# Opening a two-layer encoder by channel pairs, with the masks of its mLSTM on VectorE

## The chip, the cores and the metric

One core of one Trainium2 chip runs the kernel. The metric is the device time of one execution in microseconds (us). Five engines work side by side: TensorE (PE in the profile; PEld is its weight load), VectorE (DVE), ScalarE (ACT), GpSimd (POOL), and SyncE (SP), which here issues the DMAs.

## The reference, cut to what matters

Two independent sequences (a prompt of 256 tokens and a sample of 512, width 1024) go through two layers. Each layer's modulation (shift, scale and gate, for its mixer and its feed-forward part) comes from a condition vector. The first layer's mixer is a two-directional mLSTM with four heads of 256, the second's is a windowed attention; a convolutional feed-forward part follows each.

```python
def trunk(x, c, ...):
    for l in range(DEPTH):
        mod = jax.nn.silu(c) @ adaln_w[l] + adaln_b[l]
        sh1, sc1, g1, sh2, sc2, g2 = [t[:, None, :] for t in jnp.split(mod, 6, axis=-1)]
        h = rmsnorm(x, norm_g[l, 0]) * (1 + sc1) + sh1
        y = mlstm_mixer(h, ...)      # layer 0; swa_mixer in layer 1
        x = x + g1 * y
        h = rmsnorm(x, norm_g[l, 1]) * (1 + sc2) + sh2
        x = x + g2 * conv_ffn(h, ...)
    return rmsnorm(x, final_g)
```

In the mLSTM, `proj = h @ w_in` gives queries, keys, values, an output gate and, per head and direction, an input and a forget gate. With F the running sum of log forget gates, a = input gate - F and M the running maximum of a, the scores of a head are (k.q) * exp(a_s - M_t), for s up to t in one direction and from t on in the other. The kernel computes each direction as one masked matrix. Its outputs are divided by max(|sum of scores|, exp(-(F + M))), the two directions are added, and each head's row of 256 is normalised by its root mean square, scaled by `head_g` and multiplied by sigmoid(o).

## The kernel before, in words

The activations lie with channels on partitions: eight channel blocks `c` or `k` of 128, and 768 columns, prompt's 0 to 256 and the sample's 256 to 768. `SEQS` names the two sequences, q = 0 the sample and q = 1 the prompt; `RANGES` cuts the columns into three: r0 (256:512) and r1 (512:768) of the sample, r2 the prompt. Every matmul with a large weight is done on split operands: a high part in fp32r (`whi`, `hh`, a ScalarE cast) and a low part (`wlo`, `hl`, a VectorE subtraction), with three products hi x hi, hi x lo, lo x hi. `fp_copy_split` (L268) is the cast at L272 and the subtraction at L273. In the trace `hh` is `zh` and `hl` is `zl`. `split` (L287) makes a weight's parts of 128x1024 out of a `raw` tile, which `load` (L284) fetches with a DMA of 512 KB from SyncE's queue. The `raw` ring has 5 buffers, `whi` and `wlo` 3 each, the slabs (12 KB a partition) 6. TensorE's output goes to two sets of four PSUM banks, `ps` and `pa`.

`first` (L1561) opens the kernel. It loads the sample's x, streams the first third of the layer's modulation weights (`adaln`, L401: 16 chunks of 512 KB, each multiplied with the condition in `silc`), and meanwhile scales the two sample ranges by their RMS factors (`Norm`, L90, with `scaled`, L569). `adaln` ends with the copies of the result to `sb` (L431, L432; `sb` is a tile of the `raw` ring), four transposes (L435), shift and scale (`mod`, L442) and the gain (L445). Then `modulate` (L574) makes `hh` and `hl` of both ranges: eight modulations on VectorE (L578) and eight splits for each.

`mlstm` (L667) follows. It splits the first two query weights, loads prompt's x, squares prompt's channels on ScalarE (L111) and puts all eight sums of squares on TensorE (`Norm(..., KC)`, `pa<-inv,nt` in the trace). Prompt's RMS factor (its power is L160 on GpSimd) is spread over the partitions by TensorE (`pa<-kct,nr`) and applied in `modulated` (L561, L563, L564). `window` (L323) runs the gate weight and the two query weights over r0, r1 and r2: 3 x 3 x 8 x 3 matmuls of 256 columns. The decay follows (L699 to L716): log forget gates, running sums and maxima as scans on VectorE, and M written to DRAM.

For each head, M is broadcast from DRAM into a slab `mb` (L732). GpSimd adds the two masks for all blocks into its other half (L734). Queries and keys come from `gemmT`, values from `gemmN` (L344). For each of six score blocks ScalarE makes the exponentials (L793 to L797), and VectorE multiplies them with the scores (L798, L799). Then come the outputs: the products with the values, the denominator (L841 to L845), the two directions' sum `hs` (L846, L847), its square (L849). A half head (one sequence) closes with a power on GpSimd (L852), the scale (L855), transposes (L859) and the head's weight into `hsT` (L863).

Between these products two generators do other work step by step. `fillp` (`adaln_g`, L455) is the rest of the first layer's modulation, four groups of eight steps, on TensorE, with loads through the `raw` ring. `fill` (`adaln_v`, L497) is the second layer's, on VectorE (L516, L518). Head 0 takes four steps of `fillp` (two before the outputs of each half), heads 1 to 3 eleven each.

What sets the order: the code gives every instruction its priority, and a planner lets each engine take the first in this order that is ready in its own account of time and buffers. So the order on an engine can differ from the code's. A ring hands its buffers out in the code's order. Within an engine the order is then fixed: what waits holds up what stands behind it.

Of the kernel before, what the change touches and what calls it, by code (L numbers as in the profile page):

```python
# [16 lines left out]
P = 128  # L17
# [162 lines left out]
class Net:  # L180
# [116 lines left out]
    def ahead(self, u, h):  # L297

        self.early[u, h] = self.split(self.load(u, h))
# [44 lines left out]
    def gemmN(self, u, evac):  # L344

        ws = []
        for _, (hi, lo) in self.halves(u):
            ws.append((hi.rearrange("p (k m) -> p k m", k=4), lo.rearrange("p (k m) -> p k m", k=4)))
        for t in range(T // P):
# [50 lines left out]

    def adaln(self, l, th):  # L401
# [16 lines left out]
        ps = self.ps()  # L418
        for i in range(2 * KC):
            k, h = divmod(i, 2)  # L420
            cur = fetch(i)
            for g in range(2):
                r0 = 32 * (2 * h + g)
                self.mm(
                    ps[r0 : r0 + 32, :], self.silc[:, k, :], cur[:, g * 512 : (g + 1) * 512], k == 0, k == KC - 1
                )
# [4 lines left out]
        nc.vector.tensor_copy(sb[0], ps[:, :256])  # L431
        nc.scalar.copy(sb[1], ps[:, 256:])  # L432
        pt = self.ps()
        for b in range(4):
            nc.tensor.transpose(  # L435
                pt[:, b * P : (b + 1) * P], sb[b // 2][:, (b % 2) * P : (b % 2 + 1) * P], self.ident
            )
# [5 lines left out]
        if th == 0:  # L443
            for s in range(2):
# [52 lines left out]
    def adaln_v(self, l, pool):  # L497
# [9 lines left out]
        for grp, k in rows:  # L507
# [5 lines left out]
            for s in range(2):  # L513
                w = self.silc[:, k, s : s + 1]
                if k == 0:
                    nc.vector.tensor_scalar(acc[:, s], row, w, None, ALU.mult)  # L516
# [56 lines left out]

    def modulate(self, xt, rng, l, i):  # L574
        c0, c1, q = rng
        for c in range(KC):
            x = xt[c // 4][:, c % 4, c0:c1]
            self.nc.vector.tensor_scalar(  # L578
                x, x, self.gain[l][i][:, c, q : q + 1], self.mod[l][:, 24 * i + c, q : q + 1], ALU.mult, ALU.add
            )  # L580
            self.fp_copy_split(self.hh[:, c, c0:c1], self.hl[:, c, c0:c1], x)
# [85 lines left out]
    def mlstm(self, pool, gw, xt):  # L667
# [27 lines left out]
        for c in range(KC):  # L695
            norm.square(c)
        self.start(PROMPT, norm.stages())
        self.window(ws)
        nc.scalar.preload_act_table_set("natural_log_exp_and_others")  # L699
        nc.scalar.activation(ex, gf, AF.Abs)  # L700
        nc.scalar.activation(ex, ex, AF.Exp, scale=-1.0)
        nc.scalar.activation(ex, ex, AF.Ln, bias=self.ones[0:G, 0:1])
        nc.vector.tensor_scalar(lf, gf, 0.0, None, ALU.min)
        nc.vector.tensor_tensor(lf, lf, ex, ALU.subtract)
        scan = nc.vector.tensor_tensor_scan
        for s0, s1 in SEQS:
            scan(F[0:4, s0:s1], lf[0:4, s0:s1], z[0:4, s0:s1], 0.0, ALU.add, ALU.add)
            b = slice(s0, s1)
            scan(F[32:36, b][:, ::-1], lf[32:36, b][:, ::-1], z[32:36, b], 0.0, ALU.add, ALU.add)
        nc.vector.tensor_tensor(a, gi, F, ALU.subtract)  # L710
        for s0, s1 in SEQS:
            b = slice(s0, s1)
            scan(M[0:4, b], a[0:4, b], z[0:4, b], 0.0, ALU.max, ALU.add)
            scan(M[32:36, b][:, ::-1], a[32:36, b][:, ::-1], z[32:36, b], 0.0, ALU.max, ALU.add)
        md = self.dp.tile([G, T], F32, name="mrows")
        nc.sync.dma_start(md, M)  # L716
# [9 lines left out]
        hsT = [self.slab([P, 4, T]) for _ in range(2)]  # L726
        for h in range(4):

            mb = self.slab([P, 4, T])
            for d in range(2):  # L730
                r = d * 32 + h
                nc.sync.dma_start(mb[:, d], md[r : r + 1, :].to_broadcast([P, T]))  # L732
                mask = self.kct[:, (MF, MB)[d] : (MF, MB)[d] + P]
                nc.gpsimd.tensor_tensor(  # L734
                    mb[:, 2 + d].rearrange("p (t c) -> p t c", t=T6),
                    mb[:, d].rearrange("p (t c) -> p t c", t=T6),
                    mask.unsqueeze(1).to_broadcast([P, T6, P]),
                    ALU.add,
                )
            qk = []  # L740
            for i in range(2):
# [4 lines left out]
                for c, w in self.halves(U_MIN + 3 * h + i):  # L746
                    for q in range(2):
                        keep(t, i, c)(q, self.gemmT(w, q))
# [7 lines left out]
            def values():  # L756
# [4 lines left out]
                def evac(t, o):  # L761
                    self.fp_copy_split(v[:, 0, t, :256], v[:, 1, t, :256], o)
# [5 lines left out]
                self.gemmN(U_MIN + 3 * h + 2, evac)  # L768
# [7 lines left out]
            for q, (s0, s1) in enumerate(SEQS):  # L776
                n = (s1 - s0) // P
                for j in range(n):
# [12 lines left out]
                    act = nc.scalar.activation  # L791
                    if j:
# [19 lines left out]
            if h == 0:  # L812
                nc.vector.tensor_tensor(F, F, M, ALU.add)
# [899 lines left out]
```

## Time and profile before

| what | value |
|---|---|
| median of 3 runs | 1832.8 us (1829.74 to 1832.9) |
| the profiled execution | 1832.56 us |
| its span, first to last instruction | 1830.8 us |
| ScalarE's share of the span | 49% |
| GpSimd's share of the span | 26% |
| DMA moved | 184.47 MB, mean 101 GB/s |

The page gives an engine's busy time, its share of the span and its number of instructions. A matmul's end is modelled, and a busy TensorE may run at half clock. The row PEclk shows the granted clock in tenths for 40 slices of the span, where 9 stands for 90% and more. In groups of instructions, the numbers are the count, the busy time, the mean ns of one, and the engine's idle time before them with what ended it. In the timeline a row begins with its start and its time in us.

### The profile page before, as it was taken

What the parts mean: (1) busy time and instruction counts of PE and PEld (TensorE: products, weight loads), DVE (VectorE), ACT (ScalarE), POOL (GpSimd) and SP (SyncE); (2) the same over time, 40 slices, a digit from 0 to 9 for tenths busy, and PEclk for the clock granted to TensorE, in tenths of its full rate; (3) what the DMA queues carried; (4) which work ended last, traced back from release to release, by engine and by line L of the source; (5) the groups of instructions that cost most, each with busy time, mean ns of one, the idle gap of its engine ahead of it and who ended that gap; (6) DMA issues with size and microseconds to landing.
All of it is one profiled execution on the core that took longest, in us unless ns stands there. A gap on an engine that the chain in (4) does not pass through costs nothing.

```text
span 1830.8 us, 28867 instructions
## 1 busy us (share of the span) xinstructions
PE 1789.2 (98%) x11258; PEld 1653.6 (90%) x11258; DVE 1379.1 (75%) x2108; ACT 893.0 (49%) x1814; POOL 483.8 (26%) x385
## 2 busy tenths in 40 slices
PE   6999999999999999999999999999999999999998
PEld 3987887989998999999999999889989999999997
DVE  4755676886799877777777867767998777777876
ACT  4434434353556444444444566665564444444443
POOL 1001001022024333333331313430144333333321
PEclk7999999999999999999999999999999999999998
DMA  8344565546312222222222321124122222222212
GB/s 332 108 146 141 171 204 195 174 144 212 114 46 80 73 67 70 69 70 70 69 70 83 116 84 50 53 95 136 49 81 70 69 70 70 69 69 70 70 35 70
DMA packets 64244, 184.47 MB, mean 101 GB/s; under 512 B 6167, under 2 KB 23831, under 8 KB 64108
## 3 DMA queue, kind: packets, MB, share of 16 engines
q1 hardware_dynamic: 63532, 182.11, 30.3%
q8 instruction: 88, 1.44, 0.3%
q10 hardware_dynamic: 576, 0.52, 0.1%
q14 instruction: 48, 0.39, 0.1%
HBM read 176.17 MB, written 6.43 MB: 100 GB/s over the span
## 4 chain that ended last, share of the span: by engine, by line
PE 85%; DVE 5%; issue 4%; ACT 3%; DMA 1%; POOL 1%; SPq 0%; POOLq 0%; ACTq 0%; DVEq 0%
PE ps L266 27%; PE pa L266 24%; PE ps L1195 10%; PE ps L1196 10%; PE ps L1198 10%; PE pa L1034 1%; DVE wlo L273 1%; DMA slab<-in_adaln_w_dram 0%; DMA raw<-in_adaln_w_dram 0%; PE pa L1195 0%; PE pa L1196 0%; DVE ada L518 0%; ACT whi L272 0%; PE pa L1198 0%; ACT zh L1146 0%
## 5 line engine op out<-in xcount | busy, mean ns | idle before, releaser
L272 ACT CAST whi<-raw 128x1024 fp32r<-128x1024 f32 x233 | 243.8, 1049 | 332.5 <-PE pa L266 145.0
L273 DVE TENSOR_TENSOR wlo<-raw,whi 128x1024 fp32r<-128x1024 f32 x233 | 316.7, 1360 | 105.6 <-ACT whi L272 103.5
L266 PE MATMUL pa<-slab,whi 128*128 128x256 f32 (+1 forms) x1328 | 317.3, 334 | 0.0
L266 PEld LDWEIGHTS pa<-slab,whi 128*128 128x128 f32 x1328 | 230.1, 189 | 21.9 <-DVE slab L605 0.4
L605 DVE SCALAR_TENSOR_TENSOR slab<-pa,mod,slab 128x256 f32<-128x256 f32 (+1 forms) x332 | 192.7, 598 | 63.8 <-PE pa L266 63.6
L266 PE MATMUL pa<-slab,wlo 128*128 128x256 f32 (+1 forms) x664 | 212.8, 333 | 1.4 <-DVE wlo L273 1.4
L266 PE MATMUL ps<-zh,whi 128*128 128x256 f32 (+1 forms) x560 | 189.3, 339 | 2.6 <-ACT whi L272 1.9
L266 PE MATMUL ps<-zh,wlo 128*128 128x256 f32 (+1 forms) x560 | 184.1, 331 | 2.0 <-DVE wlo L273 2.0
L266 PE MATMUL ps<-zl,whi 128*128 128x256 f32 (+1 forms) x560 | 184.5, 332 | 0.5 <-DVE zl L564 0.5
L1195 PE MATMUL ps<-zh,whi 128*128 128x384 f32 x504 | 172.2, 342 | 3.8 <-ACT nt L1266 2.0
L1196 PE MATMUL ps<-zl,whi 128*128 128x384 f32 x504 | 169.9, 337 | 1.8 <-DVE zl L1152 1.8
L1198 PE MATMUL ps<-zh,wlo 128*128 128x384 f32 x504 | 169.0, 335 | 0.0
L266 PE MATMUL ps<-slab,whi 128*128 128x384 f32 (+2 forms) x656 | 163.5, 332 | 0.9 <-DVE slab L273 0.5
L266 PEld LDWEIGHTS pa<-slab,wlo 128*128 128x128 f32 x664 | 125.2, 189 | 14.3 <-DVE wlo L273 2.0
L1231 POOL TENSOR_TENSOR raw<-raw,raw 128x512 f32<-128x512 f32 x40 | 53.7, 1343 | 318.5 <-DVE wlo L273 245.8
L1447 POOL TENSOR_TENSOR slab<-slab 128x772 f32<-128x772 f32 x44 | 87.0, 1978 | 166.1 <-DVE slab L1435 154.1
L1434 DVE SCALAR_TENSOR_TENSOR slab<-slab,cstt,slab 128x771 f32<-128x771 f32 x88 | 108.9, 1239 | 26.7 <-ACT slab L1432 26.4
L266 PEld LDWEIGHTS ps<-zh,whi 128*128 128x128 f32 x560 | 107.6, 192 | 16.1 <-issue 4.4
L518 DVE SCALAR_TENSOR_TENSOR ada<-raw,silc,ada 128x1024 f32<-128x1024 f32 x84 | 110.6, 1354 | 14.6 <-DMA raw<-in_adaln_w_dram 14.4
L266 PEld LDWEIGHTS ps<-zl,whi 128*128 128x128 f32 x560 | 107.3, 192 | 12.6 <-issue 3.4
L266 PEld LDWEIGHTS ps<-slab,whi 128*128 128x128 f32 x656 | 115.2, 188 | 3.4 <-ACT whi L272 0.9
L266 PEld LDWEIGHTS ps<-zh,wlo 128*128 128x128 f32 x560 | 107.1, 192 | 12.2 <-DVE wlo L273 2.9
(295 smaller groups left out, 4292.8 us busy)
## 6 DMA issues: line engine op xcount, KB each, us to landing
raw<-in_w_dram SPq DMA_DIRECT2D x208, 512.0 KB, 3.7
raw<-in_adaln_w_dram SPq DMA_DIRECT2D x84, 512.0 KB, 4.5
slab<-in_x_dram SPq DMA_DIRECT2D x12, 512.0 KB, 6.7
slab<-in_adaln_w_dram SPq DMA_DIRECT2D x12, 512.0 KB, 10.3
slab<-mrows SPq DMA_DIRECT2D x8, 384.0 KB, 5.4
xs<-slab SPq DMA_DIRECT2D x6, 512.0 KB, 3.2
bt<-brow SPq DMA_DIRECT2D x16, 192.0 KB, 3.1
slab<-xs SPq DMA_DIRECT2D x6, 512.0 KB, 6.6
```

Source lines behind the costliest of these rows:

```text
L266: self.nc.tensor.matmul(out, lhsT, rhs, start=start, stop=stop)
L272: nc.scalar.copy(hi, src)
L273: return nc.vector.tensor_tensor(lo, src, hi.bitcast(F32), ALU.subtract)
L518: stt(acc[:, s], row, w, acc[:, s], ALU.mult, ALU.add)
L605: self.nc.vector.scalar_tensor_tensor(x, o, self.mod[l][:, gc + c, q : q + 1], x, ALU.mult, ALU.add)
L1034: nc.tensor.transpose(pp[:, ks], b.t[:, e, ks], self.ident)
L1195: mm(o, wh[:, k], hi[k], start=start and k == 0, stop=False, skip_group_check=True)
L1196: mm(o, wh[:, k], lo[k], start=False, stop=False, skip_group_check=True)
L1198: mm(o, wl[:, k], hi[k], start=False, stop=k == 3, skip_group_check=True)
L1231: tt(q[0], q[2], q[0], ALU.subtract)
L1434: stt(y[:, 1:], u[:, :-1], w(0), y[:, 1:], ALU.mult, ALU.add)
L1447: nc.gpsimd.tensor_tensor(y, y, yrow[:, j], ALU.mult)
```

## The change

The edits, in the order of the kernel:

- `adaln`: 6 plain matmuls of 128 columns (`warm`, ones times ones) are put behind the products of channel blocks 3 to 6, and one behind block 7. `sb` is a `tmp` tile and not one of the `raw` ring. The sample's gain is computed ahead of prompt's shift and scale.
- `modulate` is gone. `opening` takes its place and that of `window`, in a fixed order on TensorE, ScalarE and VectorE. It makes the operands channel pair by channel pair, modulating one block of each pair on ScalarE, and runs the first range's three weights as the pairs come, with the low parts of the weights last. Prompt's squares are added on GpSimd (`on_pe` 0), and its factor's TensorE work is put inside the second range.
- The decay is issued behind the splits of head 0's value weights.
- The masks: `max(M - a, mask)` on VectorE per diagonal block replaces GpSimd's additions, and one exponential serves both diagonal blocks.
- A half head's scale, transposes and `hsT` wait in `closing`: the first half's until the second half's outputs are issued, the second's until the next head's first product. `hs` lies in the second half of `mb`.
- Head 0 takes no step of `fillp`.
- Two VectorE operations are held behind named instructions: the first multiply of `adaln_v`'s groups behind the opening's last split, and the sum F + M behind the third block of head 0's values.

```diff
     def ahead(self, u, h):
-        self.early[u, h] = self.split(self.load(u, h))
+        hi, lo = (self.stg.tile([P, 1024], R, tag=t, name=self.nm(t), bufs=3) for t in ("whi", "wlo"))
+        self.early[u, h] = hi, lo
+        return self.fp_copy_split(hi, lo, self.load(u, h))
...
     def adaln(self, l, th):
...
-        ps = self.ps()
+        ps, pt = self.ps(), self.ps()
...
+            if h and k > 2:
+                with self.tc.issue_after(last.ins):
+                    self.warm(pt, 6 if k < KC - 1 else 1)
...
-        sb = self.stg.tile([P, 2, 256], F32, tag="raw", name=self.nm("sb"), bufs=5)
-        sb = [sb[:, z] for z in range(2)]
+        sb = [self.tmp([P, 256]) for _ in range(2)]
...
     def mlstm(self, pool, gw, xt):
...
-        ws = [(gw, gates)] + [(w, keep(qt0, 0, c)) for c, w in self.halves(U_MIN)]
+        raws = [self.load(U_MIN, h) for h in range(2)]
         self.load_x(io["x"], RANGES[2:], xt)
         nc.sync.dma_start(self.kct[:, P:], io["kc"][:, P : 3 * P])
-        norm = Norm(self, xt, PROMPT, self.modulated(0, 0), KC)
-        for c in range(KC):
-            norm.square(c)
-        self.start(PROMPT, norm.stages())
-        self.window(ws)
+        self.opening(xt, gw, raws, (gates, keep(qt0, 0, 0), keep(qt0, 0, 1)))
...
-                nc.gpsimd.tensor_tensor(
-                    mb[:, 2 + d].rearrange("p (t c) -> p t c", t=T6),
-                    mb[:, d].rearrange("p (t c) -> p t c", t=T6),
-                    mask.unsqueeze(1).to_broadcast([P, T6, P]),
-                    ALU.add,
-                )
...
-                self.gemmN(U_MIN + 3 * h + 2, evac)
+                self.gemmN(U_MIN + 3 * h + 2, evac, None if h else (decay, maxima))
...
+                    for d, base in ((1, j * P), (0, nb)):
+                        nc.vector.scalar_tensor_tensor(
+                            E[:, base : base + P], mb[:, d, ks], (af, ab)[d], self.kct[:, (MF, MB)[d] : (MF, MB)[d] + P],
+                            ALU.subtract, ALU.max,
+                        )
                     if j:
                         act(E[:, : j * P], mb[:, 1, s0 : s0 + j * P], AF.Exp, bias=ab, scale=-1.0)
-                    act(E[:, j * P : nb], mb[:, 3, ks], AF.Exp, bias=ab, scale=-1.0)
-                    act(E[:, nb : nb + P], mb[:, 2, ks], AF.Exp, bias=af, scale=-1.0)
+                    act(E[:, j * P : nb + P], E[:, j * P : nb + P], AF.Exp, scale=-1.0)
...
-                self.step(self.fillp, 2)
+                self.step(self.fillp, 2 if h else 0)
...
-                    hs = pool.tile([P, 256], F32, tag="hs", name=self.nm("hs"), bufs=4)
+                    hs = mb[:, 2 + ti // 3, ti % 3 * 256 : ti % 3 * 256 + 256]
...
+                while closing:
+                    closing.pop()()
...
+                closing.append(lambda *a, h=h, hq=hq, ss=ss, t0=t0, t1=t1, s0=s0, s1=s1: close(h, hq, ss, t0, t1, s0, s1))
...
+    def opening(self, xt, gw, raws, sinks):
...
+        low = lambda i: tt(lo[i], raws[i], hi[i].bitcast(F32), ALU.subtract)
+        high = lambda i: nc.scalar.copy(hi[i], raws[i])
...
+        norm = Norm(self, xt, r2, keep_factor, 0)
...
+        def operands(rng, *between):
+            made, cast, lower = sample(rng)
+            made(0)
+            made(1)
+            made(2)
+            cast(0)
+            cast(1)
+            for c in range(0, KC, 2):
+                lower(c)
+                if c + 2 < KC:
+                    cast(c + 2)
+                lower(c + 1)
+                if c + 4 < KC:
+                    made(c + 4)
+                if c + 2 < KC:
+                    made(c + 3)
+                    cast(c + 3)
+                if c < 2 * len(between):
+                    between[c // 2]()
...
+        with self.tc.manual_schedule(engines={eng.PE, eng.Activation, eng.DVE}):
...
+            with self.tc.issue_after(self.turned.ins):
+                self.warm(bank[0, 0], 5)
+            high(0)
+            operands(r0)
+            high(1)
+            low(0)
+            low(1)
+            squares(0)
+            for c in range(0, KC, 2):
+                for k in (c, c + 1):
+                    three(r0, 0, k)
+                for k in (c, c + 1):
+                    mm(r0, 1, 0, 0, k)
+                    mm(r0, 1, 0, 1, k)
+            for c in range(KC):
+                mm(r0, 2, 0, 0, c)
+                mm(r0, 2, 0, 1, c)
+            for i in (1, 2):
+                for c in range(KC):
+                    mm(r0, i, 1, 0, c, c == KC - 1)
+
+            operands(r1, lambda: squares(4))
+            for c in range(0, KC, 2):
+                if c == 4:
+                    next(factor)
+                if c == 6:
+                    next(factor, None)
+                for i in range(3):
+                    for k in (c, c + 1):
+                        three(r1, i, k)
...
+            for c in range(KC):
+                if c + 1 < KC:
+                    ts[c + 1] = first(c + 1)
+                if c == 2:
+                    sinks[0](0, bank[0, 0])
...
+                three(r2, 0, c)
+                three(r2, 1, c)
+            for c in range(KC):
+                three(r2, 2, c)
+            self.opened = self.ahead(U_MIN + 1, 0)
+            for i in (1, 2):
+                sinks[i](0, bank[i, 0])
+        for i in range(3):
+            sinks[i](1, bank[i, 1][:, :256])
...
-        for rng in RANGES[:2]:
-            self.modulate(xt, rng, 0, 0)
```

`mm(rng, i, z, a, c)` is one product of weight i (its high part for z = 0, its low part for z = 1) with the operand's high (a = 0) or low part, `three` the three products of a channel block, `made` a modulation (odd blocks on ScalarE, even ones on VectorE), `cast` and `lower` the operand's two parts, and `first(c)` prompt's multiply with gain and factor and its activation.

More of the change, by code (lines that the diff above doesn't have):

```diff
@@ L348, in gemmN @@
             ws.append((hi.rearrange("p (k m) -> p k m", k=4), lo.rearrange("p (k m) -> p k m", k=4)))
+        for f in then or ():
+            f()
         for t in range(T // P):
@@ L398, in save_x, with warm @@
             self.nc.sync.dma_start(dst[:, 4 * i : 4 * i + 4, c0:c1], xt[i][:, :, c0:c1])
+    def warm(self, o, n):
+        for _ in range(n):
+            self.mm(o[:, :P], self.ones, self.ones, True, True)
     def adaln(self, l, th):
@@ L442, in adaln @@
             nc.vector.tensor_tensor(dst[:, :, :, s], src[:, :, :, s], ab, ALU.add)
-        if th == 0:
-            for s in range(2):
+            if th == 0:
                 nc.vector.scalar_tensor_tensor(
@@ L700, in mlstm @@
[L700 to L709, printed above, removed]
```

151 lines of the change are left out of this document (110 added, 41 removed).

## The prediction

> **What bounds the kernel now.** I read the page's shares first. The three lines are the span, the busy time of each engine, and the clock that TensorE was granted in 40 slices.
>
> ```profile
> span 1830.8 us, 28867 instructions
> ...
> PE 1789.2 (98%) x11258; PEld 1653.6 (90%) x11258; DVE 1379.1 (75%) x2108; ACT 893.0 (49%) x1814; POOL 483.8 (26%) x385
> ...
> PEclk7999999999999999999999999999999999999998
> ```
>
> TensorE is busy 98% of the span, and the clock is short of full speed in the first slice and almost nowhere else. So a change that takes no matmuls out of the long middle can win only where TensorE waits, runs at half clock, or does work that another engine could do. Next come the waits of TensorE between 36 and 160 us (what waited, for whom, total, times, longest), and stretches of the window view (length, busy time and count of PE, PEld, DVE, ACT, POOL, then granted clock, DMA share, GB/s).
>
> ```profile
> PE pa L266 <- ACT hs L846: 1.6, 1, 1.6
> PE ps L266 <- ACT whi L272: 1.6, 1, 1.6
> PE pa L859 <- ACT hs L855: 1.2, 1, 1.2
> PE ps L266 <- DVE wlo L273: 0.6, 1, 0.6
> PE ps L266 <- DVE slab L273: 0.4, 1, 0.4
> PE ps L266 <- DVE slab L276: 0.4, 1, 0.4
> ```
>
> ```profile
> 23.90:34.10 10.20, 10.06 (x40) 4.67 (x44) 3.82 (x10) 1.04 (x1) 1.69 (x3) 0.50 1.04 398
> 36.00:48.00 12.00, 11.73 (x58) 11.32 (x57) 11.83 (x35) 9.01 (x25) 1.19 (x1) 0.57 0.55 212
> 48.00:72.00 24.00, 24.00 (x201) 23.95 (x200) 18.57 (x33) 11.80 (x20) 2.09 (x1) 1.00 0.29 93
> 122.00:130.00 8.00, 5.88 (x21) 4.36 (x20) 7.54 (x11) 1.79 (x7) 0.00 (x0) 0.79 0.78 284
> 160.00:420.00 260.00, 257.79 (x1800) 222.88 (x1800) 192.96 (x316) 108.95 (x276) 23.13 (x18) 1.00 0.52 175
> ```
>
> Until 34 us the DMA share is 1.04: the modulation weights stream in, and nothing in the change makes them fewer. From 36 to 48 us TensorE looks 98% busy, yet gets through 58 matmuls in 12 us at a clock of 0.57, against 201 in the next 24 us. After 160 us it loses about 2 us in 260. So three places are worth something: the opening at 36 to 48 us, the stretch 122 to 130 us, and the three waits near 145 to 152 us. The timeline shows the opening.
>
> ```profile
> 34.81 0.42 DVE L431 COPY sb<-ps 128x256 f32<-128x256 f32 x1 [0.42 <-PE ps L266]
> 36.38 0.25 DVE L445 SCALAR_TENSOR_TENSOR gain<-mod,cstt 128x8 f32<-128x8 f32 x2
> 36.58 5.26 DVE L578 TENSOR_SCALAR slab<-slab,gain,mod 128x256 f32<-128x256 f32 x16
> 37.48 0.55 PE L266 MATMUL ps<-zh,whi 128*128 128x256 f32 x1 [0.18 <-ACT zh L272]
> 38.13 5.28 PE L266 MATMUL pa<-inv,nt 128*128 128x2 f32 x24
> 43.27 0.56 PE L266 MATMUL ps<-zh,whi 128*128 128x256 f32 x1
> ```
>
> The gain is known at 36.6 us, VectorE then modulates all 16 pieces before the first low part, and TensorE spends 5.3 us on prompt's sums of squares, two columns each. The window's stream starts only at 43.27, and at half clock.
>
> **The opening, step by step.** The window (three weights, three ranges, eight channels, three products) has 216 matmuls, which these groups between 37 and 72 us confirm (the groups with zl and wlo have the same counts: 3 x 48 + 3 x 24).
>
> ```profile
> L266 PE MATMUL ps<-zh,whi 128*128 128x256 f32 x48 | 14.7, 312 | 0.2 <-ACT zh L272 0.2
> L266 PE MATMUL pa<-zh,whi 128*128 128x256 f32 x24 | 6.8, 283 | 0.0
> ```
>
> One at full clock takes 24.0/201 = 0.12 us, so 216 need 25.9 us. Before, 24 of them were done by 48 us, and the other 192 with 4 of the factor's take 23.5 us: the window ends at 71.5 us. Afterwards the work per pair of channels is priced by these rows (eight low parts of 0.35, casts of 0.33, prompt's multiply and its activation of 0.41 each; a whole weight's cast and its low part).
>
> ```profile
> 41.76 2.43 DVE L273 TENSOR_TENSOR zl<-slab,zh 128x256 fp32r<-128x256 f32 x7
> 38.90 1.61 ACT L272 CAST zh<-slab 128x256 fp32r<-128x256 f32 x5
> 51.92 3.22 DVE L561 SCALAR_TENSOR_TENSOR nt<-slab,gain,pa 128x256 f32<-128x256 f32 x8 [2.38 <-issue]
> 40.42 1.04 ACT L272 CAST whi<-raw 128x1024 fp32r<-128x1024 f32 x1
> 44.10 1.22 DVE L273 TENSOR_TENSOR wlo<-raw,whi 128x1024 fp32r<-128x1024 f32 x1
> ```
>
> A pair costs VectorE one modulation (5.26/16 = 0.33) and two low parts, 1.03 us, and ScalarE one modulation (priced as the 0.41 activation) and two casts, 1.05 us. TensorE spends 10 matmuls, 1.2 us, on a pair in its first pass, so at full clock it and not the supply sets the pace. With the gain at about 36.3 (the first sample's gain no longer waits for the second's mod), modulation, cast and low part take 1.0 us: the stream starts at 37.2. Behind it VectorE owes two weight low parts (1.22 each) before item 1's low pass, 56 matmuls or 6.7 us later; it is done by about 43.1. The second range begins near 46.3 and its operands from 43.1 on. Prompt's squares go to GpSimd and leave 4 TensorE records instead of 32. They and the factor's 4 add 0.9 us, so the window ends at 37.2 + 25.9 + 0.9 + 0.3 (prompt's supply, 0.80 a channel on VectorE against 0.72 on TensorE) = 64.3 us: **7.2 us** won.
>
> Two things must hold. First, the first weight's cast now stands ahead of everything on ScalarE, in a fixed order, so its load must land before 36 us. The queue's rows (start, time, issues) say when.
>
> ```profile
> 18.71 4.34 SPq L415 DMA_DIRECT2D slab<-in_adaln_w_dram  x4
> 24.01 1.65 SPq L392 DMA_DIRECT2D slab<-in_x_dram  x2
> 29.86 15.81 SPq L281 DMA_DIRECT2D raw<-in_w_dram  x6
> ...
> SPq L281 <- PE ps L435: 4.1, 1, 4.1
> ```
>
> The code has the two weights ahead of prompt's x, yet they are issued behind it: `sb` takes a buffer of the raw ring between them, and a later load indeed waits for the transposes that read `sb`. With `sb` elsewhere they move ahead of prompt's 1 MB. At 0.4 MB/us (398 GB/s) that is 2.6 us sooner, some 35 us. If they don't move, that is a rival.
>
> Second, the clock must stay up. The 36 to 48 us row shows that the sums with two columns count for little, as the clock stays near half while TensorE looks busy; the new 128-column matmuls at 19 to 33 us and five behind the transposes are there instead. This row is the price of two such matmuls (two records each) at half clock.
>
> ```profile
> 30.40 1.22 PE L266 MATMUL pa<-kct,nr 128*128 128x128 f32 x4
> ```
>
> Six take up to 3.7 us, more than the two loads that they lie beside (2 x 1.3 us, 512 KB each at 0.4 MB/us), and half of that at full clock; so they may delay the end of the modulation. Bounds: 1.3 us sooner (the last tail at full clock) to 1.7 us later (one stretch of 3.4 us at half clock); I take nothing, nearest to the old 34.8.
>
> [...]
>
> The factor's power is in range two. It took 3.29 us here, beside a busy VectorE.
>
> ```profile
> 28.89 0.71 POOL L160 TENSOR_TENSOR nr<-nr,mhalf 128x2 f32<-128x2 f32 x1 [3.93 <-DVE nr L159]
> 46.81 3.29 POOL L160 TENSOR_TENSOR nr<-nr,mhalf 128x2 f32<-128x2 f32 x1 [17.21 <-DVE nr L159]
> ```
>
> TensorE has 18 matmuls (2.2 us) between the sums and the spread, which stand in its fixed order, so the stall is 0 to 1.5 us. I take 0, because VectorE has then no operand left to make. K's first split hides under item 2's 24 matmuls (2.9 us against 1.04 + 1.22).
>
> **Head 0.** It loses four steps of the modulation, hence their loads and matmuls. These rows show what they cost.
>
> ```profile
> 118.76 7.66 SPq L281 DMA_DIRECT2D raw<-in_adaln_w_dram  x4
> ...
> 123.72 1.04 ACT L272 CAST whi<-raw 128x1024 fp32r<-128x1024 f32 x1 [1.04 <-DMA raw<-in_w_dram]
> ```
>
> The next head's weight arrives late behind them; TensorE waits 1.6 + 0.6 us, and the clock falls to 0.79 over 8 us (1.7 us). Together 3.9 us. But the steps' matmuls also filled holes between the score blocks; I charge 1.0 us for them, though the next head's queries, now loaded early, can fill them. **2.9 us** won, bounds 0 to 3.9. The four steps come later: by the code 33 calls remain for 32 steps, the last in head 3's outputs, where the same late weight may return (0 to 3.9 us; I take 0, as TensorE loses 2 us in all between 160 and 420 us).
>
> Later closings take the transposes from behind a scale that isn't ready, and free two of the four `pa` banks. Of the waits 1.2, 1.6 and 0.4 all three may go; the 1.6 hangs on VectorE's queue too, so I take **2.4 us** (0 to 3.2). The scaled halves now live in the maxima's slab, which is held until the next head's first product; queries and keys free two slabs earlier, so I cost that at nothing. Without that cover the next head's keys wait for the outputs' end.
>
> **Masks.** 48 small VectorE operations take the place of eight on GpSimd and 24 activations. No row shows this one; its neighbours have this size.
>
> ```profile
> L273 DVE TENSOR_TENSOR nt<-E,nt 128x128 fp32r<-128x128 f32 x8 | 2.0, 283 | 0.0
> L734 POOL TENSOR_TENSOR slab<-slab,kct 128x768 f32<-128x768 f32 x8 | 16.1, 2023 | 51.9 <-DMA slab<-mrows 41.9 <-PE pa L266 9.9
> ```
>
> 48 x 0.28 = 13.6 us on VectorE, which between 160 and 420 us idles 260 - 193 = 67 us. Behind each mask on that queue stand the products, splits and weights' low parts. Bounds at the end of the kernel: -0.4 us (GpSimd's 2 us per mask leaves the chain) to 13.6; I take **1.0 us lost**, by the row of low parts that TensorE waited for (0.6).
>
> **Sum:** -7.2 - 2.9 - 2.4 + 1.0 = -11.5 us. The profiled execution took 1832.56 (1.76 outside its span), a hair under the median 1832.8: 1832.6 - 11.5 = **1821.1 us**.
>
> **Rivals.**
> 1. *The clock falls in the opening.* For: the row at 36 to 48 us, and the idle 35 to 37 us that remains. Two stretches at half clock (6.8 us) pass 32 matmuls instead of 57: 3.0 us, so 1824.1.
> 2. *Head 0's stalls move instead of going.* For: VectorE's long operations hold its queue, and the filling matmuls are gone. 2.9 + 2.4 come back: 1826.4.
> 3. *The change's first step doesn't take place:* the weights stay behind prompt's x and land at 38.5 (half a queue later). ScalarE blocks until 39.5, the stream starts at 40.4 and at half clock for 4 us (1.7 us), ending at 40.4 + 0.4 + 1.7 + 26.9 = 69.4; with the stalls kept, 1830.5. Against: the wait for `sb`'s reader.
> 4. *Slower: VectorE becomes the bound in heads 1 to 3.* Place: products and low parts behind the masks. It decides if VectorE's idle can't be used because everything it waits for comes at once; then all 13.6 us show and head 0 wins nothing: 1832.6 - 7.2 + 13.6 = 1839.0. Against: 67 us idle.
>
> **How the numbers follow.** Forecast 0.48, clock 0.17, stalls 0.15, no earlier load 0.08, VectorE 0.12. A measurement of this kernel tells about 0.2% (3.7 us) from no change. Below 1828.9 lie the forecast and rivals 1 and 2: faster 0.80; rival 3 is the same, 0.08; slower 0.12. The range goes from 1814.5 (all bounds good: 1.3 + 1.0 + 0.8 + 1.4 + 2.1 below the forecast, the last the idle after 160 us) to 1831 (rival 3 inside), and leaves out rival 4.
>
> **What would show it.** Right: window's stream from 37 us at clock 1.00, no `pa<-inv,nt` group of 24, the window's last matmul near 64 us, no wait for `whi` by DMA in head 0, no wait `pa L859 <- ACT hs L855`, masks of 0.28 us. Wrong: a cast of `whi` waiting for DMA past 36 us, a clock under 0.8 between 36 and 48, TensorE waiting for `E` or `wlo` in heads 1 to 3.

## The result and the profile after

| kernel | median of the runs | lowest to highest | ratio to before, 95% interval |
|---|---|---|---|
| before | 1832.8 us (7 runs) | 1829.74 to 1835.66 | 1 |
| changed | 1827.06 us (7 runs) | 1823.31 to 1829.86 | 0.9968 (0.9956 to 0.998) |
| changed, measured again beside the experiments | 1824.37 us (6 runs) | 1821.74 to 1826.56 | 0.9958 (0.9942 to 0.9975) |

The change makes the kernel faster, by 5.7 us in the first series and 8.1 us in the second (whose runs of before have the median 1832.46); the intervals overlap. 1821.1 us was forecast, 11.5 us below before. The time lies inside the range, near the second rival (1826.4). The profiled execution of the changed kernel took 1823.31 us, the lowest of its seven. First its page: span, busy time of each engine, granted clock in 40 slices.

```profile
span 1821.4 us, 28979 instructions
...
PE 1785.9 (98%) x11290; PEld 1652.4 (91%) x11290; DVE 1390.6 (76%) x2148; ACT 891.4 (49%) x1798; POOL 474.1 (26%) x384
...
PEclk9999999999999999999999999999999999999998
```

TensorE still sets the span, VectorE's busy time rose by 11.5 us, and the first slice is now at full clock. Next the stretches of the window view, in the columns of before's.

```profile
36.00:48.00 12.00, 11.70 (x94) 11.16 (x93) 10.34 (x24) 10.94 (x27) 3.42 (x3) 1.00 0.70 244
48.00:72.00 24.00, 23.72 (x173) 22.17 (x172) 18.67 (x35) 16.88 (x33) 4.01 (x5) 1.00 0.20 63
122.00:130.00 8.00, 8.00 (x57) 7.46 (x56) 4.42 (x10) 2.71 (x11) 0.00 (x0) 1.00 0.41 133
135.00:146.00 11.00, 7.87 (x47) 4.30 (x47) 5.10 (x14) 6.88 (x21) 0.72 (x1) 0.69 0.01 2
160.00:420.00 260.00, 258.15 (x1816) 222.60 (x1817) 201.44 (x350) 104.06 (x260) 23.96 (x18) 1.00 0.59 191
```

Two of the three places that the prediction named are mended: from 36 to 48 us the clock is 1.00, and from 122 to 130 us TensorE no longer idles. But a new hole stands at 135 to 146 us: TensorE is busy for 7.87 of 11 us, at a clock of 0.69. The waits of TensorE between 36 and 160 us name it.

```profile
PE ps L266 <- DVE slab L276: 2.4, 1, 2.4
PE pa L736 <- ACT slab L732: 0.8, 1, 0.8
PE ps L266 <- ACT zh L946: 0.3, 1, 0.3
```

The waits for the next head's weight (1.6 and 0.6 us) are gone, and so is the one of 1.6 us for `hs` (L846). The transposes still wait for the scale, 0.8 us and not 1.2: L736 was L859, and the scaled half is now part of a slab. A single wait of 2.4 us for an evacuation of the queries is new, of which 0.4 us stood before. Another new one, of 1.5 us for the cast of the keys, stands just behind these rows, ahead of head 1's first score at 163.3 us. Cut at stages that both kernels have, the span of the two profiled executions differs like this (the window's end is the start of its last matmul):

| from, to | before | changed | difference |
|---|---|---|---|
| start to the window's end | 71.4 us | 66.3 us | -5.1 |
| to the first score product of head 1 | 101.9 us | 97.0 us | -4.9 |
| to the second layer's first attention outputs | 926.5 us | 928.8 us | +2.3 |
| to the end | 730.9 us | 729.3 us | -1.6 |

The third row pays back part of the second: by the code, the four steps taken from head 0 run there. So in these two profiles head 0's edits and the masks together are worth 2.6 us, not the 4.3 us of the forecast. The last row lies in code that the change doesn't touch: in before's second layer TensorE waited 1.4 us in three waits for `zl`, in the changed kernel 0.4 us in two. In the changed kernel's second profile the same stretch takes 730.3 us.

### The profile page after: what moved, and what is told of

Same layout as the page of the kernel before. It is cut to its first block, busy times and chain, and to the rows that moved or that the text cites. A ratio compares the mean times of both kernels' runs of the same rounds, so it can differ in the third digit from the quotient of the medians.

```text
span 1821.4 us, 28979 instructions
## 1 busy us (share of the span) xinstructions
PE 1785.9 (98%) x11290; PEld 1652.4 (91%) x11290; DVE 1390.6 (76%) x2148; ACT 891.4 (49%) x1798; POOL 474.1 (26%) x384
## 4 chain that ended last, share of the span: by engine, by line
PE 87%; DVE 5%; ACT 3%; DMA 3%; issue 1%; POOL 1%; SPq 0%; POOLq 0%; DVEq 0%; ACTq 0%
PE ps L266 28%; PE pa L266 24%; PE ps L1348 10%; PE ps L1351 10%; PE ps L1349 10%; DMA raw<-in_w_dram 1%; PE pa L1187 1%; DMA raw<-in_adaln_w_dram 1%; DVE wlo L273 1%; ACT whi L272 1%; DMA slab<-in_adaln_w_dram 0%; PE pa L1349 0%; PE pa L1348 0%; DVE wlo L1473 0%; DVE ada L528 0%
```

## The experiments

The expectations were written before each run. Times are medians; experiments 1 to 4, 5 to 7 and 8 to 11 were made beside runs of before of their own (medians 1832.18, 1832.46 and 1832.98 us). The ratio is to these.

### 1. The opening alone

Before's kernel with the new opening (with `adaln`'s extra matmuls, `sb` outside the ring and the loads ahead); decay, masks, closings and steps as before.

```diff
-        self.window(ws)
+        self.opening(xt, gw, raws, (gates, keep(qt0, 0, 0), keep(qt0, 0, 1)))
```

> Before, with the opening's part of the change alone (opening in pairs, the extra matmuls, sb outside the raw ring, adaln_v held behind the opening); masks on GpSimd, closings at once, four steps in head 0. Theory (the gain is the opening's): the window ends near 66.5 us as in the changed kernel's trace (71.6 before), and 1827 to 1828 us, all or nearly all of the change's gain. Rival (the gain lies in head 0's parts): within 2 us of 1832.8.

Measured: 1836.86 us, ratio 1.0029 (1.0018 to 1.0041): slower. Yet the window ends at 65.6 us, as it should. The timeline of this kernel shows where the time goes.

```profile
80.50 1.22 DVE L273 TENSOR_TENSOR wlo<-raw,whi 128x1024 fp32r<-128x1024 f32 x1
81.64 0.94 DVE L705 TENSOR_TENSOR slab<-slab,slab 36x768 f32<-36x768 f32 x1
...
87.87 0.84 ACT L809 ACTIVATE slab<-slab 36x768 f32<-36x768 f32 x1 [11.43 <-DVE slab L754]
88.62 1.58 ACT L272 CAST slab<-ps 128x512 fp32r<-128x512 f32 x4
...
89.24 1.22 PE L266 MATMUL pa<-slab,slab 128*128 128x512 f32 x2 [6.05 <-ACT slab L272]
```

ScalarE's next instruction, the exponential of the sum F + M, belongs to the decay and waits 11.43 us for VectorE's scans and that sum behind them; the keys' cast stands behind it, and TensorE waits 6.05 us for that cast. Half clock follows: from 92.8 to 95.2 us matmuls of 256 columns start 0.21 us apart, from 95.5 us on 0.12 us, and the mean clock from 66 to 160 us is 0.89. In this order the scores also come ahead of head 0's values, so they need the decay at once. The theory that the opening brings its 7 us by itself falls.

### 2. The rest alone

The changed kernel with before's `adaln`, `modulate` and `window`.

```diff
-        self.opening(xt, gw, raws, (gates, keep(qt0, 0, 0), keep(qt0, 0, 1)))
+        norm = Norm(self, xt, PROMPT, self.modulated(0, 0), KC)
+        for c in range(KC):
+            norm.square(c)
+        self.start(PROMPT, norm.stages())
+        self.window(ws)
```

> The change without its opening: the window, the modulation and sb as before; masks on VectorE, later closings, no steps in head 0, the decay behind the value weights. Theory (head 0 wins 4 us by the loads and loses as much or more where the next head's queries wait for a slab behind the late closing): 1831 to 1836 us, a TensorE wait of 2 us or more after the first half's transposes. Rival (head 0's parts win by themselves): 1828 or less.

Measured: 1831.79 us, ratio 0.9999 (0.999 to 1.0008): no difference. Its waits of TensorE in 36 to 160 us begin with these.

```profile
PE ps L266 <- DVE slab L276: 2.4, 1, 2.4
PE ps L266 <- DVE slab L273: 1.6, 1, 1.6
PE pa L745 <- ACT slab L741: 0.8, 1, 0.8
```

The 2.4 us and the 0.8 us of the changed kernel are there without the opening: they come from head 0's edits, and they use up what these win.

### 3. `hsT` written early

The slabs are handed out in the code's order, and a slab is taken at its first write. The first write of the first sequence's `hsT` is in the closing of head 0's first half, which the change moves behind the second half's outputs. The slabs that the code asks for later, the next head's `mb` and queries, then stand behind that closing. One VectorE column written ahead of head 0 takes the slab early and is the only edit.

```diff
+                nc.vector.memset(hsT[0][:, 0, 0:1], 0.0)
```

> The changed kernel with one added VectorE memset of one column of hsT[0] ahead of head 0's scores, so that this slab is handed out there and not at the first late closing. Theory (slabs are handed out in order, and head 1's queries stand behind hsT's): the four evacuations of head 1's queries start some 15 us sooner than 137 us, TensorE's wait of 2.4 us for them and the half clock at 138 to 145 us go, 4 to 7 us faster than the changed kernel, some 1821 us. Rival (TensorE simply has no other work there): no difference, 1827.

Measured: 1820.63 us (1818.74 to 1822.62), ratio 0.9937 (0.9925 to 0.9949), 6.4 us below the changed kernel's first series and 3.7 us below its second, whose interval overlaps with this one. First the changed kernel's timeline at the hole, then the windows of this one.

```profile
133.76 1.24 PE L266 MATMUL pa<-slab,nt 128*128 128x258 f32 x9
...
135.20 1.70 ACT L732 ACTIVATE slab<-slab,ss 128x256 f32<-128x256 f32 x4
...
135.76 1.63 PE L736 MATMUL pa<-kct,slab 128*128 128x128 f32 x8 [0.75 <-ACT slab L732]
...
137.16 1.63 ACT L275 ACTIVATE slab<-ps 128x512 fp32r<-128x512 f32 x4
137.32 0.75 DVE L740 TENSOR_SCALAR slab<-pa,cstt 128x512 f32<-128x512 f32 x1 [1.61 <-PE pa L736]
...
139.03 1.61 DVE L276 SCALAR_TENSOR_TENSOR slab<-ps,slab 128x512 fp32r<-128x512 f32 x3
...
139.77 0.65 PE L266 MATMUL ps<-raw,silc 128*32 128x256 f32 x4 [2.38 <-DVE slab L276]
```

```profile
66.00:160.00 94.00, 94.00 (x622) 82.06 (x622) 68.33 (x129) 43.50 (x99) 1.71 (x2) 1.00 0.42 132
135.00:146.00 11.00, 11.00 (x71) 9.69 (x68) 3.79 (x12) 5.89 (x18) 1.71 (x2) 1.00 0.00 1
```

In the changed kernel the next head's queries are complete in their `ps` banks, but the order on the engines puts their evacuation behind the closing: its ScalarE part (L275) behind the scale (L732), its VectorE part (L276) behind the `hsT` writes (L740), which wait for the transposes (L736). TensorE has no bank until 139.77, and from 138.4 to 145.3 us its clock is 0.50. With the slab taken early the last of these evacuations starts at 131.2 us and TensorE has no hole from 66 to 160 us; the clock is 1.00 from 36 to 600 us. The theory of the slab queue holds.

### 4. No extra matmuls

```diff
-        for _ in range(n):
+        for _ in range(0):
```

> The changed kernel without the extra 128-column matmuls (none while the modulation streams, none behind the transposes); nothing else changes. Theory (they hold the clock): half clock somewhere between 36 and 48 us, the window's 216 matmuls take 3 us longer or more, 1830 us. Rival (the clock would be up anyway, and they only delay the modulation's end): the modulation ends up to 1 us sooner and the kernel is as fast or 1 us faster, 1826 to 1827.

Measured: 1823.67 us, ratio 0.9953 (0.994 to 0.9965), like the changed kernel. Windows and wait:

```profile
36.00:48.00 12.00, 11.07 (x89) 10.91 (x90) 11.01 (x23) 10.94 (x28) 4.34 (x4) 1.00 0.73 261
```

```profile
PE ps L266 <- ACT zh L946: 1.4, 1, 1.4
```

The clock is 1.00 without them, so that the rival holds: the opening without the two-column sums keeps it up by itself. In this pair of profiles the modulation's end is reached 1.2 us sooner without the extra matmuls (its transposes at 34.6 us against 35.8), and the window starts at 36.9 us. Only 0.1 us of this lies behind the last modulation load; the load itself lands at 32.9 us and not at 33.9. It lands between 32.9 and 33.3 us in the four profiles without the extra matmuls (before and experiments 2, 4 and 9) and between 33.2 and 34.7 us in the ten with them. So the price goes from nothing to about 1.5 us, and why the load lands later isn't shown.

### 5. The changed kernel again, and `sb` back in the ring

> The changed kernel once more, beside the others of this set on one chip. Both theories: 1824 to 1829 us. By the slab theory its trace has again the four evacuations of head 1's queries in a row behind the first late closing, near 137 us, with a TensorE wait of over 2 us and the clock at half in the stretch after it.

Measured: 1824.37 us; the waits of 2.4 and 0.8 us are there again.

```diff
-        sb = [self.tmp([P, 256]) for _ in range(2)]
+        sb = self.stg.tile([P, 2, 256], F32, tag="raw", name=self.nm("sb"), bufs=5)
+        sb = [sb[:, z] for z in range(2)]
```

> The changed kernel with sb in the raw ring, as before. Theory (sb's place in the ring is what held the first weights behind prompt's x): the first weight lands 3 to 4 us later, near 39 us, ScalarE's first cast of the opening waits for it, the window starts near 41 us instead of 38 and ends near 69.5 us or later, 1830 us or more. Rival (the load's place doesn't hang on sb, or ScalarE isn't late by it): window from 38 us, 1827.

Measured: 1828.34 us, ratio 0.9978 (0.9968 to 0.9988), 4.0 us above the changed kernel. The two queues (first the changed kernel's, in its second series), then the waits with `sb` in the ring:

```profile
23.91 1.60 SPq L281 DMA_DIRECT2D raw<-in_w_dram  x2
26.41 1.66 SPq L396 DMA_DIRECT2D slab<-in_x_dram  x2
```

```profile
24.07 1.66 SPq L396 DMA_DIRECT2D slab<-in_x_dram  x2
26.62 4.70 SPq L695 DMA_DIRECT2D kct<-in_kc_dram  x1
31.43 5.98 SPq L281 DMA_DIRECT2D raw<-in_w_dram  x5
```

```profile
PE ps L266 <- ACT zh L947: 2.7, 1, 2.7
```

`sb` decides on which side of prompt's x the two weights are issued. Behind it, the window runs from 40.8 to 70.0 us instead of 38.1 to 66.4, and the clock from 36 to 48 us is 0.86, some 3.4 us at half. This is the third rival, and it prices what kept it away.

### 6. Closings at once

```diff
-                closing.append(lambda *a, h=h, hq=hq, ss=ss, t0=t0, t1=t1, s0=s0, s1=s1: close(h, hq, ss, t0, t1, s0, s1))
+                close(h, hq, ss, t0, t1, s0, s1)
```

> The changed kernel with each half head closed at once, as before. Theory (the late closing costs more by the slab queue than it wins): the wait for the evacuated queries (2.4 us) and the half clock behind it go, waits for the scaled hs of 1 to 3 us come back, 1823 to 1826 us, 1 to 4 faster than the changed kernel. Rival (late closings are a gain by themselves): 1829 or more.

Measured: 1825.32 us, ratio 0.9967 (0.9955 to 0.9979), 1.0 us above the changed kernel, which the intervals don't tell apart.

```profile
PE pa L736 <- ACT slab L732: 2.6, 1, 2.6
PE pa L266 <- ACT slab L871: 0.6, 1, 0.6
PE ps L266 <- DVE slab L276: 0.5, 1, 0.5
```

At once, TensorE waits 2.6 us for the scale; late, it waits 2.4 us for the queries' bank. As the change has it, closing late wins about nothing: the wait has moved.

### 7. Head 0's steps back

```diff
-                self.step(self.fillp, 2 if h else 0)
+                self.step(self.fillp, 2)
```

> The changed kernel with two steps of the modulation again before each half of head 0's outputs. Theory (their loads stand ahead of head 1's weights in SyncE's queue and make them late): a TensorE wait of 1 us or more for a weight's cast in head 0, 1829 to 1831 us. Rival (the steps fill TensorE where it waits, and cost nothing): 1825 to 1827.

Measured: 1827.56 us, ratio 0.9972 (0.9962 to 0.9982), 3.2 us above the changed kernel, with overlapping intervals. Two of its four kinds of waits from 100 to 200 us (the others, 0.3 and 0.2 us, are for `dn`):

```profile
PE pa L736 <- ACT slab L732: 3.5, 3, 1.6
...
PE ps L266 <- DVE wlo L273: 0.3, 1, 0.3
```

The size is that of the forecast (2.9), the mechanism isn't: TensorE waits for the scale of the closings, and no cast waits for a late weight.

### 8. The opening with the decay moved

Experiment 1, but with the decay behind the splits of head 0's value weights and the sum F + M held behind the third block of the values, both as in the change. Masks, closings and steps are before's.

```diff
-                self.gemmN(U_MIN + 3 * h + 2, evac)
+                self.gemmN(U_MIN + 3 * h + 2, evac, None if h else (decay, maxima))
```

> The opening's part together with the decay's move behind head 0's value weights; masks on GpSimd, closings at once and four steps in head 0 as before. Theory (the opening alone was slower because the decay stood ahead of the evacuation of head 0's keys, and TensorE waited 6.0 us there and fell to half clock): no wait over 2 us between 70 and 100 us, the scores of head 0 start near 101 us, 1826 to 1830 us, 7 or more below the opening alone. Rival (the opening needs the loads or closings of the change in head 0, not the decay's move): 1834 or more.

Measured: 1825.77 us, ratio 0.9963 (0.9952 to 0.9976): 11.1 us below experiment 1, 7.2 below before. Its longest waits in 36 to 160 us are those of head 0's end, none of them at 70 to 100 us.

```profile
PE pa L736 <- ACT hs L732: 2.5, 1, 2.5
PE ps L266 <- ACT whi L272: 1.0, 1, 1.0
PE ps L266 <- DVE slab L276: 0.8, 1, 0.8
```

So the opening and the decay's place are one step. They carry most of the whole change. The hold on F + M came with the decay here, and the instruction that blocked ScalarE in experiment 1 hangs on this sum; which of the two moves is needed isn't shown.

### 9. `hsT` early and no extra matmuls

Experiments 3 and 4 together.

> The changed kernel with hsT[0] handed out early and without the extra 128-column matmuls. Theory (by now: the opening without the two-column sums holds the clock by itself): as with them, 1819 to 1822 us, clock at full from 20 us on. [...]

Measured: 1818.34 us (1817.55 to 1823.13), ratio 0.9924 (0.9912 to 0.9937). The clock is 1.00 from 20 to 34.1 us and from 36 to 600 us, the window ends at 65.6 us. It is a version that beats both kernels; that it beats experiment 3 isn't shown by these intervals.

### 10. and 11. The masks, on GpSimd and twice

Both on experiment 3, where TensorE has no hole in head 0 that could hide them. First GpSimd's additions and two exponentials as before; then every mask on VectorE issued twice (the second writes the same values).

```diff
+                    nc.gpsimd.tensor_tensor(
+                        mb[:, 2 + d].rearrange("p (t c) -> p t c", t=T6),
...
-                    for d, base in ((1, j * P), (0, nb)):
-                        nc.vector.scalar_tensor_tensor(
...
-                    act(E[:, j * P : nb + P], E[:, j * P : nb + P], AF.Exp, scale=-1.0)
+                    act(E[:, j * P : nb], mb[:, 3, ks], AF.Exp, bias=ab, scale=-1.0)
+                    act(E[:, nb : nb + P], mb[:, 2, ks], AF.Exp, bias=af, scale=-1.0)
```

> The changed kernel with hsT[0] handed out early and the masks added by GpSimd into the maxima's slab as before (hs follows them in the same half of the slab). Theory (the scores' chain is hidden, so masks are worth little either way): 1819 to 1824 us, within 3 us of the early hsT[0] alone. Rival (VectorE's queue is tight, and 13.6 us off it show): 1817 or less.

Measured: 1821.51 us, ratio 0.9938 (0.9926 to 0.995), 0.9 us above experiment 3, which the intervals don't tell apart. Its profiled execution, the slowest of its six (1825.53 us), shows all the same how long VectorE's operations took beside the additions on GpSimd.

```profile
116.06 4.27 POOL L753 TENSOR_TENSOR slab<-slab,kct 128x768 f32<-128x768 f32 x2 [10.44 <-DMA slab<-mrows]
116.17 2.48 DVE L273 TENSOR_TENSOR PT<-E,PT 128x640 fp32r<-128x640 f32 x1
118.57 2.85 DVE L528 SCALAR_TENSOR_TENSOR ada<-raw,silc,ada 128x1024 f32<-128x1024 f32 x1
...
122.28 0.37 DVE L724 COPY eT<-pa 128x216 f32<-128x216 f32 x1
...
122.70 0.58 PE L266 MATMUL pa<-slab,PT 128*128 128x258 f32 x1 [3.17 <-DVE eT L724]
```

Beside the two additions for head 1, VectorE's low part of the scores (`PT`) takes 2.48 us and a multiply of `adaln_v` (`ada`) 2.85 us; in experiment 3's head 0 they take 0.82 and 1.28 us in the mean. The copy to `eT` stands behind them, TensorE waits 3.17 us for it, and the clock is at half for 3.4 us from 122.4 us on (0.98 from 66 to 160 us). Experiment 3 has no such wait, and its clock there is 1.00.

```diff
+                    for d, base in ((1, j * P), (0, nb)):
+                        nc.vector.scalar_tensor_tensor(
+                            E[:, base : base + P], mb[:, d, ks], (af, ab)[d], self.kct[:, (MF, MB)[d] : (MF, MB)[d] + P],
+                            ALU.subtract, ALU.max,
+                        )
```

> The changed kernel with hsT[0] handed out early and each VectorE mask computed twice into the same place: 48 more operations of some 0.28 us. Theory (VectorE has the room): 0 to 3 us over the early hsT[0] alone, 1820 to 1824. Rival (VectorE is the bound in the heads): 8 to 14 us more, 1828 to 1834.

Measured: 1816.31 us (1815.03 to 1817.03), ratio 0.9908 (0.9896 to 0.9921): 4.3 us faster than experiment 3, which no theory had. The first line is the mask's view in the changed kernel (least, median, most ns of one), then TensorE's waits behind 1214 us in experiment 3 and in this one.

```profile
L813 DVE SCALAR_TENSOR_TENSOR E<-slab,aT,kct x48: 339/346/352, 102.0 to 337.6; 128x128 f32<-128x128 f32 x48
```

```profile
PE ps L1350 <- DVE zl L1306: 1.2, 3, 0.8
...
PE pa L136 <- ACT nt L111: 1.0, 1, 1.0
```

```profile
PE ps L1355 <- DVE zl L1311: 0.4, 2, 0.2
...
PE pa L136 <- ACT nt L111: 0.2, 1, 0.2
```

48 operations of 0.346 us add up to 16.6 us. Masks in a row start only 0.26 us apart, so they overlap in part, and VectorE's busy time rises by 9.4 us (1389.1 to 1398.5). The last attention outputs of the second layer nevertheless start at 1213.8 us in experiment 3 and at 1214.0 us here, so the doubling costs about nothing. The profiled executions differ by 2.2 us, all of it behind that point: 1.6 us are these two waits, far from any mask. TensorE's order differs from head 0 on; the planner has the second mask in its account. Why that ends in shorter waits in the second layer, and why the medians differ by more, stays open.

One cut through all profiled executions (each a single one, in us) shows what such differences are worth.

| kernel | window's end | from there to the last attention outputs | from there to the end |
|---|---|---|---|
| before | 71.4 | 1156.4 | 602.9 |
| changed | 66.3 | 1153.8 | 601.3 |
| changed, second series | 66.4 | 1153.6 | 602.4 |
| 1, opening alone | 65.6 | 1168.6 | 603.3 |
| 2, the rest alone | 70.0 | 1156.5 | 603.5 |
| 3, `hsT` early | 66.0 | 1147.8 | 603.2 |
| 6, closings at once | 66.7 | 1152.0 | 604.5 |
| 7, head 0's steps back | 66.9 | 1156.9 | 604.1 |
| 8, opening and decay | 66.5 | 1156.6 | 600.9 |
| 10, masks on GpSimd | 67.0 | 1152.6 | 604.2 |
| 11, masks twice | 66.7 | 1147.3 | 600.8 |

No edit touches the code of the last column, and it still goes from 600.8 to 604.5 us. So 2.0 of the 6.8 us by which experiment 8's profile is ahead of before's aren't the opening's; 5.0 us are. In the middle column the early `hsT` is worth about 5.9 us, and the masks on GpSimd cost 4.8 us against experiment 3.

## Why the prediction was right, and where it failed

**The opening (-7.2).** Right in mechanism, measured at 5.1 us up to the window's end. The stream starts at 38.0 us and not at 37.2, and it lasts 28.3 us and not 27.1. The changed kernel's timeline shows the start.

```profile
36.05 1.05 ACT L907 CAST whi<-raw 128x1024 fp32r<-128x1024 f32 x1
...
36.89 0.25 DVE L454 SCALAR_TENSOR_TENSOR gain<-mod,cstt 128x8 f32<-128x8 f32 x2
37.10 0.60 ACT L942 ACTIVATE slab<-slab,mod,gain 128x256 f32<-128x256 f32 x1
...
38.04 0.39 PE L266 MATMUL ps<-zh,whi 128*128 128x256 f32 x1 [0.28 <-ACT zh L946]
```

The weight's cast is ahead of the gain, as the prediction wanted. But the first modulations start at 37.10 us and not at the 36.3 us taken, and this 0.8 us is the whole delay of the stream (36.3 and 1.0 make 37.3, not 37.2). It lies within the bounds of the term that I set to nothing, the modulation's end beside the extra matmuls; the last load landed 0.9 us later than before, and experiment 4 doesn't settle whether the matmuls are the cause. ScalarE's modulation takes 0.60 us and not 0.41. The stream's extra 1.2 us is spread over the three ranges.

**The clock.** The outcome was forecast (1.00 against 0.57), for a reason that is half wrong. Experiments 4 and 9 have no extra matmul and the same clock; an opening without the 5.3 us of two-column sums is enough. With the sums in (experiment 2) the clock from 36 to 48 us is 0.72; that it is the sums and not the rest of that opening was the author's estimate, as no run changes them alone. The first rival, a clock that falls in the opening, came only where the weights were late (experiment 5). The stretches at half clock last 3.41 us (before, from 126.30 us), 6.83 us (the changed kernel, from 138.44) and 10.24 us (before, from 23.90 and from 37.55). The prediction's stretch of 3.4 us, and the first rival's two (6.8 us), are of the length of the first.

**The weights ahead of prompt's x.** Right: issued at 24.51 and landed at 35.19 us in the changed kernel's profile, 29.86 and 38.47 us before. Experiment 5 puts 4.0 us on it.

**The decay.** It had no term in the sum, and this was luck: experiments 1 and 8 differ by 11.1 us, so the opening's gain hangs on its place and on the hold on F + M.

**The masks (+1.0).** What VectorE takes on costs about nothing (experiment 11); one mask takes 0.346 us and not 0.28, but in a row they start 0.26 us apart. What the term left out is that VectorE's operations can take longer beside the additions on GpSimd (2.48 and 2.85 us against 0.82 and 1.28), so that the change may win here: by experiment 10's profile 4.8 us, by the medians 0.9 us, which isn't clear of noise. Before shows it too.

```profile
145.85 3.60 POOL L734 TENSOR_TENSOR slab<-slab,kct 128x768 f32<-128x768 f32 x2
148.24 1.23 DVE L844 TENSOR_TENSOR dn<-dn,eT 128x2 f32<-128x2 f32 x1 [3.46 <-ACT dn L841]
```

This maximum on two columns takes 0.16 us in the median. Here it ends with GpSimd's addition, and the reciprocal, `hs` (L846) and TensorE's wait of 1.6 us for it follow. The prediction put this wait to the closings and to VectorE's queue. Whether it is the masks' move that takes it away, no run shows by itself.

The fourth rival falls: from 160 to 420 us VectorE is busy for 201.44 us and not 192.96, and TensorE is idle for 1.85 us and not 2.21.

**Head 0's steps (-2.9).** Experiment 7 gives 3.2 us, with intervals that overlap; between the window's end and the last attention outputs the profiles differ by 3.3 us. That a late weight is what the steps cost isn't confirmed.

**The later closings (-2.4): the step that failed.** The prediction says: "queries and keys free two slabs earlier, so I cost that at nothing. Without that cover the next head's keys wait for the outputs' end." It counted slabs that come free and not the order in which the ring hands them out. The first `hsT` is taken at its first write, in the very step that moves late, and the next head's `mb` and queries stand behind it. The forecast's 2.4 us came back as waits of 2.4 and 0.8 us and as 6.8 us at half clock (3.4 us in the second profile). It is the second rival's outcome, with another mechanism than the one given there. Experiment 3 takes this away alone and gets 3.7 to 6.4 us back by the medians, 5.9 us by the profiles: 1820.63 us, with the closings still late.

## What to carry to other kernels

When a step is moved later, list what it allocates for the first time, and what the code asks of the same ring behind it: a ring that hands out in the code's order lets a late first write hold up buffers that have long been free. When a stage is made to end sooner, look at what its successors wait for next on a fixed queue (here the decay ahead of the keys' cast), or the gain becomes a loss. When an operation leaves an engine, look also at what ran slower beside it there. Differences of 1 to 4 us between versions of such a kernel can also come from waits that a new order makes or removes far from the edit; look for the stage before you credit the edit.

## What the runs showed of the hardware

An idle of 2.4 us, with a transpose stretch ahead of it, came with half clock for 6.8 us in the profile of the changed kernel and for some 3.4 us in its second one (0.84 from 135 to 146 us); experiment 6, whose longest wait up to 160 us is 2.6 us, shows 1.00 from 66 to 170 us. So how long the clock was down beside such an idle varied from case to case. The mean granted clock also differs between runs of one kernel: of the 51 runs of before beside the experiments, the nine at 0.988 or 0.989 have a median of 1833.0 us, the eleven at 0.993 or 0.994 one of 1830.8 us.

Some operations of VectorE and GpSimd took longer beside the other engine's in these profiles: beside GpSimd's additions three of VectorE's took 2.48, 2.85 and 1.23 us, and 0.82, 1.28 and 0.16 us otherwise (experiments 10 and 3, and before); GpSimd's power on two columns took 3.29 us at 46.81 us, beside a busy VectorE, and 0.71 us at 28.89 us (before).
